# Batched float32 matmul on one core: the first pair's loads in 8 KB runs, and no small store beside them

## The chip, the core and the metric

The kernel runs on one core of one Trainium2 chip. The metric is the device time of one execution, in microseconds (us). Before the change it was 124.75 us (median of 3 runs, 124.73 to 124.80). PE is the matrix engine and PEld its weight loads, ACT and DVE are the scalar and vector engines, POOL is a further engine, which only clears memory here, and SP is the engine that issues most DMAs here. "The DMA engines" are the 16 engines that move data for the core.

## The reference, cut to what matters

```python
batch, m, k, n = 16, 512, 512, 512          # a: (16, 512, 512), b: (16, 512, 512), float32
np.matmul(a.transpose(0, 2, 1), b)          # out: (16, 512, 512), float32
```

Two inputs of 16.8 MB are read and one output of 16.8 MB is written: 50.3 MB, none of it twice.

## The kernel before

Two batches make a pair, and there are eight pairs. A load brings one pair of a, or of b, as 2 MB: each of 128 partitions gets 16 KB that lie together in memory. DVE casts to bf16, PE multiplies into its result memory (PSUM), ACT copies PSUM to an output tile, and SP stores it, 2 MB at a time in 8 KB runs. SP issues all sixteen loads first and the eight stores after them. On ACT's queue there is one small store of 64 KB at the beginning; its place in the output is written again later.

```python
    with tc.tile_critical(no_gpsimd_drain=True):
        for n in range(2 * pairs):                      # a0, b0, a1, b1, ...
            if n >= NX:                                 # NX = 4 load buffers
                nc.sync.wait_ge(s_in, n - NX + 1)
            nc.sync.dma_start(x_ts[n % NX][:], in_v[n % 2][n // 2]).then_inc(s_x[n % NX], 16)
        nc.sync.wait_ge(s_w, 16)
        for i in range(pairs):
            nc.sync.wait_ge(s_out, i + 1)
            nc.sync.dma_start(out_v[i], o_ts[i % NO][:]).then_inc(s_o if i else s_o0, 16)
        # ... final waits; DVE casts; PE loop over pairs ...
        nc.gpsimd.memset(o_ts[0][:, 0, 0, 0:P], 0.0).then_inc(s_z, 1)
        nc.scalar.wait_ge(s_z, 1)
        nc.scalar.dma_start(out_v[0][:, 0, 0, 0:P], o_ts[0][:, 0, 0, 0:P]).then_inc(s_w, 16)
        nc.scalar.wait_ge(s_w, 16)
        # ... ACT copies PSUM to o_ts ...
```

Of the kernel before, what the change touches and what calls it, by code (L numbers as in the profile page):

```python
# [1 line left out]

# [4 lines left out]

@with_exitstack
def kernel(
    ctx: ExitStack,  # L10
    tc: tile.TileContext,
    a: bass.AP,
    b: bass.AP,
    out: bass.AP,
):
    nc = tc.nc
    P = 128
    batch, K, M = a.shape
    _, _, N = b.shape
    f32 = mybir.dt.float32  # L20
    bf = mybir.dt.bfloat16




    G = 2
    Q = P // G
    R = K // Q
    V = 2
    RV = R // V  # L30
    T = M // P
    H = T // 2
    pairs = batch // G
    in_v = [x.rearrange("(pair g) (q r) m -> pair (g q) r m", g=G, r=R) for x in (a, b)]
    out_v = out.rearrange("(pair g) (c t) n -> pair c g t n", g=G, t=T)

    NX = 4
    NO = pairs - 1



    pool = ctx.enter_context(tc.tile_pool(name="sb", bufs=1))
    psum = ctx.enter_context(tc.tile_pool(name="ps", bufs=1, space=bass.MemoryType.PSUM))
    x_ts = [pool.tile([P, R, M], f32, name=f"x{j}") for j in range(NX)]
    abf_ts = [pool.tile([P, RV, M], bf, name=f"abf{v}") for v in range(V)]
    bbf_ts = [pool.tile([P, RV, N], bf, name=f"bbf{v}") for v in range(V)]
    o_ts = [pool.tile([P, G, T, N], f32, name=f"o{j}") for j in range(NO)]
    dve_done = pool.tile([1, 2 * pairs], f32, name="dve_done")
    act_done = pool.tile([1, pairs], f32, name="act_done")
    ps_ts = [[psum.tile([P, 2, N], f32, name=f"ps{g}{h}") for h in range(H)] for g in range(G)]  # L50

    s_x = [tc.alloc_semaphore(f"s_x{j}") for j in range(NX)]
    s_o0 = tc.alloc_semaphore("s_o0")
    s_o = tc.alloc_semaphore("s_o")
    s_w = tc.alloc_semaphore("s_w")
    s_z = tc.alloc_semaphore("s_z")
    s_in = tc.alloc_semaphore("s_in")
    s_cast = tc.alloc_semaphore("s_cast")
    s_v = tc.alloc_semaphore("s_v")
    s_mm = tc.alloc_semaphore("s_mm")  # L60
    s_ev = [tc.alloc_semaphore(f"s_ev{h}") for h in range(H)]
    s_out = tc.alloc_semaphore("s_out")

    with tc.tile_critical(no_gpsimd_drain=True):  # L64
        for n in range(2 * pairs):
            if n >= NX:
                nc.sync.wait_ge(s_in, n - NX + 1)
            nc.sync.dma_start(x_ts[n % NX][:], in_v[n % 2][n // 2]).then_inc(s_x[n % NX], 16)
        nc.sync.wait_ge(s_w, 16)
        for i in range(pairs):  # L70
            nc.sync.wait_ge(s_out, i + 1)
            nc.sync.dma_start(out_v[i], o_ts[i % NO][:]).then_inc(s_o if i else s_o0, 16)
        nc.sync.wait_ge(s_o0, 16)
        nc.sync.wait_ge(s_o, 16 * (pairs - 1))

        for i in range(pairs):
            for v in range(V):
                if i and v == 0:
                    nc.vector.wait_ge(s_v, G * i)
                if i and v == 1:  # L80
                    nc.vector.wait_ge(s_mm, G * H * i)
                for n in (2 * i, 2 * i + 1):
                    if v == 0:
                        nc.vector.wait_ge(s_x[n % NX], 16 * (n // NX + 1))
                    nc.vector.tensor_copy(  # L85
                        out=(bbf_ts if n % 2 else abf_ts)[v][:],
                        in_=x_ts[n % NX][:, v * RV:(v + 1) * RV, :],
                    ).then_inc(s_cast, 1)
                    if v == V - 1:

                        nc.vector.memset(dve_done[:, n:n + 1], 0.0).then_inc(s_in, 1)  # L91

        for h in range(H):
            nc.tensor.sem_inc(s_ev[h], 1)
        with nc.tensor.Fori(0, pairs):
            for v in range(V):
                nc.tensor.wait_ge(s_cast, 2).then_inc(s_cast, -2)
                for t in range(T):
                    h = t // 2
                    if v == 0 and t % 2 == 0:  # L100
                        nc.tensor.wait_ge(s_ev[h], 1).then_inc(s_ev[h], -1)  # L101
                    for r in range(RV):
                        for g in range(G):
                            rows = slice(g * Q, (g + 1) * Q)
                            a_m = abf_ts[v][rows, r, :].rearrange("p (c t) -> p t c", t=T)
                            mm = nc.tensor.matmul(  # L106
                                ps_ts[g][h][:, t % 2, :],
                                a_m[:, t],
                                bbf_ts[v][rows, r, :],
                                start=(v == 0 and r == 0),  # L110
                                stop=(v == V - 1 and r == RV - 1),
                            )
                            if v == 0 and t == T - 1 and r == RV - 1:
                                mm.then_inc(s_v, 1)
                            if v == V - 1 and t % 2 and r == RV - 1:
                                mm.then_inc(s_mm, 1)


        nc.gpsimd.memset(o_ts[0][:, 0, 0, 0:P], 0.0).then_inc(s_z, 1)  # L119
        nc.scalar.wait_ge(s_z, 1)  # L120
        nc.scalar.dma_start(out_v[0][:, 0, 0, 0:P], o_ts[0][:, 0, 0, 0:P]).then_inc(s_w, 16)
        nc.scalar.wait_ge(s_w, 16)
        for i in range(pairs):
            if i == NO:
                nc.scalar.wait_ge(s_o0, 16)
            for h in range(H):
                for g in range(G):
                    nc.scalar.wait_ge(s_mm, G * H * i + G * h + g + 1)  # L128
                    ev = nc.scalar.copy(  # L129
                        out=o_ts[i % NO][:, g, 2 * h:2 * h + 2, :], in_=ps_ts[g][h][:]  # L130
                    )
                ev.then_inc(s_ev[h], 1)

            nc.scalar.memzero(act_done[:, i:i + 1]).then_inc(s_out, 1)  # L134


# [1 line left out]
_INS = ['a', 'b']  # L138
_OUTS = [((16, 512, 512), 'float32')]


# [23 lines left out]
```

## Time and profile before

| what | value | view |
|---|---|---|
| time, median | 124.75 us | runs |
| span of the profiled execution | 122.8 us | page |
| DMA queue of SP, share of 16 engines' span | 96.9% | queue table |
| PE, DVE, ACT busy | 49%, 31%, 26% | busy table |
| last work of PE, DVE or ACT | ends near 93 us | chain of waits |

The page of the kernel before. The first two rows cut the span into 40 slices: busy tenths of the DMA engines, and what they moved. Then the DMA queues, with packets, MB and share.

```profile
DMA  4999999999999999999999999999999999999992
GB/s 85 386 415 437 432 437 443 427 432 437 427 432 427 427 427 427 427 427 427 427 427 427 427 427 427 427 416 427 424 427 427 427 427 427 427 427 427 429 432 101
...
q1 hardware_dynamic: 4480, 50.33, 96.9%
q10 hardware_dynamic: 144, 0.07, 0.2%
```

The DMA engines are full from the second slice to the last but one; this is the bound. The Trainium skill, "DMA: Bandwidth & Descriptors", section "Where 436 GB/s comes from", puts the ceiling at 435.2 GB/s; the 427 of most slices agree with it. So an engine that computes faster would bring nothing. What can still move are the two ends, and what each DMA engine has to carry.

The start of the kernel before, as windows. The columns are the stretch, its length, busy time with count for PE, PEld, DVE, ACT and POOL, granted clock, DMA share and GB/s.

```profile
1.00:2.00 1.00, 0.00 (x0) 0.00 (x0) 0.00 (x0) 0.00 (x0) 0.15 (x1) 1.00 0.24 49
2.00:3.00 1.00, 0.00 (x0) 0.00 (x0) 0.00 (x0) 0.00 (x0) 0.00 (x0) 1.00 0.98 180
3.00:4.00 1.00, 0.00 (x0) 0.00 (x0) 0.00 (x0) 0.00 (x0) 0.00 (x0) 1.00 0.73 262
4.00:6.00 2.00, 0.00 (x0) 0.00 (x0) 0.00 (x0) 0.00 (x0) 0.00 (x0) 1.00 1.00 426
```

Between 2 and 4 us the engines have work but move little: the first packets are slow. And the start of the timeline of the kernel before (start, duration, engine, line, operation; in brackets how long the engine sat idle before, and what ended that):

```profile
0.94 0.39 SPq L68 DMA_DIRECT2D x<-in_a_dram  x1
1.18 0.37 ACTq L121 DMA_DIRECT2D out_dram<-o  x1
...
8.90 1.23 DVE L85 CAST abf<-x 128x2048 bf16<-128x2048 f32 x1 [8.90 <-DMA x<-in_a_dram]
13.79 1.23 DVE L85 CAST bbf<-x 128x2048 bf16<-128x2048 f32 x1 [3.66 <-DMA x<-in_b_dram]
```

The trace also holds one record for every DMA packet: start, duration, size and queue. It does not name the DMA engine. But each DMA ends on every engine with a 4-byte write to its semaphore, so each DMA has 16 such writes, one for each engine. This gives, after each DMA, when the last engine got there. For the end of the kernel these are the 16 writes of the last store. In before, the last one starts at 121.05 us. The records show the time from one packet to the next on an engine: 607 ns with 16 KB loads, 306 ns with 8 KB stores, and 630 ns where a 512-byte packet of the small store lies between two 16 KB packets.

### The profile page before, as it was taken

Reading aid. Unit: us, or ns where it says so; the run is one execution under the profiler, and the core shown is the slowest. Engines: PE = TensorE matmul, PEld = TensorE weight load, DVE = VectorE, ACT = ScalarE, POOL = GpSimd, SP = SyncE. Lnnn points to the kernel's source line nnn. Section 1 sums busy time; section 2 is a strip of 40 time slices with the busy share of each in tenths; the row PEclk is TensorE's granted clock in tenths of the full one; section 3 lists DMA queues with packets and bytes.
Section 4 is the critical chain, followed back from the end, with each engine's and each line's share of the span. In section 5 each row is a group of like instructions: output and inputs, shape, how many; then the busy total and the mean of one; then the engine's idle time right before and its main releaser. Section 6 shows DMA issues by size and latency. Waiting matters only on the chain. (4 is left out here: it accounts for less than half of the span.)

```text
span 122.8 us, 1258 instructions
## 1 busy us (share of the span) xinstructions
PE 60.2 (49%) x512; PEld 35.4 (29%) x512; DVE 37.9 (31%) x48; ACT 31.8 (26%) x41; POOL 0.4 (0%) x5
## 2 busy tenths in 40 slices
PE   0000099859769649829919928997960000000000
PEld 0000045436446336416606604544630000000000
DVE  0012562583294094174355337239000000000000
ACT  0000000690740830650570390065093000000000
POOL 1000000000000000000000000000000000000000
PEclk9999999999999999999999995999998555555555
DMA  4999999999999999999999999999999999999992
GB/s 85 386 415 437 432 437 443 427 432 437 427 432 427 427 427 427 427 427 427 427 427 427 427 427 427 427 416 427 424 427 427 427 427 427 427 427 427 429 432 101
DMA packets 4624, 50.40 MB, mean 410 GB/s; under 512 B 400, under 2 KB 528, under 8 KB 528
## 3 DMA queue, kind: packets, MB, share of 16 engines
q1 hardware_dynamic: 4480, 50.33, 96.9%
q10 hardware_dynamic: 144, 0.07, 0.2%
HBM read 33.55 MB, written 16.84 MB: 410 GB/s over the span
## 5 line engine op out<-in xcount | busy, mean ns | idle before, releaser
L106 PE MATMUL ps<-bbf,abf 64*128 64x512 bf16 x512 | 60.2, 392 | 30.7 <-PEq L101 29.0
L106 PEld LDWEIGHTS ps<-bbf,abf 64*128 64x128 bf16 x512 | 35.4, 112 | 55.1 <-issue 38.2
L129 ACT COPY o<-ps 128x1024 f32<-128x1024 f32 x32 | 30.1, 1027 | 38.7 <-PE ps L106 38.7
L85 DVE CAST abf<-x 128x2048 bf16<-128x2048 f32 x16 | 19.6, 1223 | 25.1 <-PE ps L106 16.2
L85 DVE CAST bbf<-x 128x2048 bf16<-128x2048 f32 x16 | 19.6, 1224 | 22.9 <-DMA x<-in_b_dram 22.9
L129 ACT ACT_TABLE_LOAD x1 | 1.3, 1283 | 22.6 <-PE ps L106 22.6
L134 ACT ACTIVATE act_done<-act_done 1x1 uint32<-1x1 uint32 x8 | 1.6, 197 | 0.0
L91 DVE MEMSET dve_done<- 1x1 f32 x16 | 0.9, 59 | 0.0
L119 POOL MEMSET o<- 128x128 f32 x1 | 0.2, 204 | 0.5 <-SPq L64 0.5
L149 POOL MEMSET const-bfloat16-1.0<- 128x1 bf16 x1 | 0.1, 102 | 0.0
L149 POOL MEMSET const-uint8-127<- 128x1 uint8 x1 | 0.1, 101 | 0.0
L149 POOL MEMSET const-float32-0.0<- 128x1 f32 x1 | 0.1, 98 | 0.2 <-issue 0.2
L149 POOL MEMSET const-float32-1.0<- 128x1 f32 x1 | 0.1, 98 | 0.0
## 6 DMA issues: line engine op xcount, KB each, us to landing
x<-in_a_dram SPq DMA_DIRECT2D x8, 2048.0 KB, 12.2
x<-in_b_dram SPq DMA_DIRECT2D x8, 2048.0 KB, 16.0
out_dram<-o SPq DMA_DIRECT2D x8, 2048.0 KB, 30.6
out_dram<-o ACTq DMA_DIRECT2D x1, 64.0 KB, 9.0
```

The costliest lines, as they stand in the source:

```text
L85: nc.vector.tensor_copy(out=(bbf_ts if n % 2 else abf_ts)[v][:], in_=x_ts[n % NX][:, v * RV:(v + 1) * RV, :],).then_inc(s_cast, 1)
L91: nc.vector.memset(dve_done[:, n:n + 1], 0.0).then_inc(s_in, 1)
L106: mm = nc.tensor.matmul(ps_ts[g][h][:, t % 2, :], a_m[:, t], bbf_ts[v][rows, r, :], start=(v == 0 and r == 0), stop=(v == V - 1 and r == R ...
L119: nc.gpsimd.memset(o_ts[0][:, 0, 0, 0:P], 0.0).then_inc(s_z, 1)
L129: ev = nc.scalar.copy(out=o_ts[i % NO][:, g, 2 * h:2 * h + 2, :], in_=ps_ts[g][h][:])
L134: nc.scalar.memzero(act_done[:, i:i + 1]).then_inc(s_out, 1)
L149: nc = _bacc.Bacc("TRN2", target_bir_lowering=False, num_devices=1)
```

## The change

The intent: take the small store's packets out of the way of the first loads, and let the first loads come in shorter packets.

```diff
-            nc.sync.dma_start(x_ts[n % NX][:], in_v[n % 2][n // 2]).then_inc(s_x[n % NX], 16)
-        nc.sync.wait_ge(s_w, 16)
+            if n < 2:
+                for v in range(V):                      # V = 2 halves of RV = 4 rows
+                    r = slice(v * RV, (v + 1) * RV)
+                    nc.sync.dma_start(x_ts[n][:, r, :], in_v[n][0][:, r, :]).then_inc(s_x[n], 16)
+            else:
+                nc.sync.dma_start(x_ts[n % NX][:], in_v[n % 2][n // 2]).then_inc(s_x[n % NX], 16)
...
-                        nc.vector.wait_ge(s_x[n % NX], 16 * (n // NX + 1))
+                        nc.vector.wait_ge(s_x[n % NX], 16 * (n // NX + 1 + (n % NX < 2)))
...
-        nc.gpsimd.memset(o_ts[0][:, 0, 0, 0:P], 0.0).then_inc(s_z, 1)
-        nc.scalar.wait_ge(s_z, 1)
-        nc.scalar.dma_start(out_v[0][:, 0, 0, 0:P], o_ts[0][:, 0, 0, 0:P]).then_inc(s_w, 16)
-        nc.scalar.wait_ge(s_w, 16)
```

(The two semaphores s_w and s_z go as well.)

More of the change, by code (lines that the diff above doesn't have):

```diff
@@ L54 @@
     s_o = tc.alloc_semaphore("s_o")
-    s_w = tc.alloc_semaphore("s_w")
-    s_z = tc.alloc_semaphore("s_z")
     s_in = tc.alloc_semaphore("s_in")
```

## The prediction

> **What bounds the kernel now.** The DMA engines. The page's slices show DMA at 9 tenths or more from the second slice to the last but one, at 386 to 443 GB/s; the queue table gives the SP queue 96.9% of 16 engines' span, against 49% for PE and 31% for DVE. In 4 us windows from 4 to 120 us the rate stays within 406 to 455 GB/s, through loads and stores (from about 81 us) alike. The Trainium skill ("DMA: Bandwidth & Descriptors", Where 436 GB/s comes from) puts the ceiling at 435.2 GB/s; the trace agrees, with about 427. PE, DVE and ACT are done by 93 of 122.8 us. So only three things matter: when the DMA engines start, what each moves, and what it loses on the way.
>
> **An engine's budget, from the trace's packet records.** First packets start at 1.98 to 2.5 us (first issue at 0.94). In steady state a 16 KB load packet follows its predecessor after 607 ns, an 8 KB store packet after 306 ns, a 4-byte semaphore write takes about 6 ns: 128 x 607 + 128 x 306 + 24 x 6 = 117.0 us. The engines end at 120.4 to 121.1. The remaining 1.3 us or so lie in the first 4 us: the first 16 KB packets take 0.9 to 2.0 us instead of 0.61, some second ones 0.7 to 1.1, and the window from 3 to 4 us moves only 262 GB/s at a DMA share of 0.73.
>
> **What the change does.**
> 1. Small store gone: 128 packets of 512 B, 8 per engine. From 4.7 us they alternate with load packets (the same page, Queues, rings and completion order: round-robin by packet) and stretch the interval from 607 to 630 ns. 8 x 23 = 0.18 us saved on every engine, all critical. The waits for it cost nothing now: it landed at about 10 us; ACT's first copy starts at 23.9 us, SP's first store issue is at 66.8.
> 2. First pair in 8 KB packets: per engine 32 packets for 16. At 306 against 303.5 ns that costs 16 x 4.5 = 0.07 us, plus 2 more semaphore writes, 0.01 us. SP issues 6 DMAs instead of 4, about 0.45 us each, but the queue is 15 us ahead.
> 3. Start-up: first packets half as long, so an engine that fills its pipe packet by packet may lose up to 0.3 us less. I count 0.15 us, the uncertain term.
> 4. The casts do not start earlier than about 8.6 us (8.9 before): the first still waits for both halves of a. Not critical.
>
> Sum: -0.18 + 0.08 - 0.15 = -0.25 us.
>
> **Prediction: 124.5 us**, 8 in 10 between 124.0 and 124.9. Chances: faster by over 2% 0.01, within 2% 0.98, slower by over 2% 0.01.
>
> **What would show it.** The ACT queue (q10) gone from the queue table; intervals of 607 or 2 x 306 ns between 4 and 10 us and no 512 B packets; first packets ending earlier, and the window 3 to 4 us above 262 GB/s; last packets at about 120.8 instead of 121.1 us; the later rate unchanged. Step 3 is wrong if no more bytes have moved by 5 us than before.
>
> **What would make it wrong.** If the small store warmed the write path, the first real stores near 81 us show packets well over 306 ns, and up to about 1 us comes back. If the three engines that end 0.35 us after the rest get later by start-up luck, the saving vanishes; likewise if half-row reads are slower at the start. A large effect needs a change of the steady rate; I see no cause.

## The result, and the profile after

The changed kernel took 124.79 us (median of 6 runs, 124.64 to 124.86), and before 124.78 us (6 runs). The ratio is 1.000, with a 95% interval from 0.9987 to 1.0013. A ratio here is the mean time of one kernel's fast runs over the mean of the other's in the same rounds, so it is not quite the ratio of the medians. The time lies inside the predicted range, but so would that of a kernel that changes nothing; the predicted quarter of a microsecond is not there.

The page of the changed kernel, the same rows:

```profile
DMA  3999999999999999999999999999999999999991
GB/s 77 406 427 427 440 432 438 427 427 438 427 432 427 427 427 432 432 427 427 432 438 427 427 427 427 427 398 427 424 430 427 427 430 427 430 430 427 427 432 59
...
q1 hardware_dynamic: 4768, 50.33, 96.9%
```

ACT's queue is gone, SP's has 288 packets more (256 more of data, 32 more of semaphore writes), and the last slice moves 59 instead of 101 GB/s: most engines finish earlier. The windows and the timeline of the start of the changed kernel:

```profile
1.00:2.00 1.00, 0.00 (x0) 0.00 (x0) 0.00 (x0) 1.00 (x1) 0.00 (x0) 1.00 0.06 16
2.00:3.00 1.00, 0.00 (x0) 0.00 (x0) 0.00 (x0) 0.18 (x1) 0.00 (x0) 1.00 0.92 197
3.00:4.00 1.00, 0.00 (x0) 0.00 (x0) 0.00 (x0) 0.00 (x0) 0.00 (x0) 1.00 0.92 360
4.00:6.00 2.00, 0.00 (x0) 0.00 (x0) 0.00 (x0) 0.00 (x0) 0.00 (x0) 1.00 1.03 430
```

```profile
0.94 0.87 SPq L70 DMA_DIRECT2D x<-in_a_dram  x2
...
8.50 1.23 DVE L88 CAST abf<-x 128x2048 bf16<-128x2048 f32 x1 [8.50 <-DMA x<-in_a_dram]
13.47 1.23 DVE L88 CAST bbf<-x 128x2048 bf16<-128x2048 f32 x1 [3.75 <-DMA x<-in_b_dram]
```

What was predicted for the start is there. The window from 3 to 4 us moves 360 instead of 262 GB/s, and the first cast starts 0.40 us earlier. (The prediction's own test, more bytes moved by 5 us, says little: 1.00 against 0.99 MB, counted by packets started, and a packet is 8 or 16 KB on each of 16 engines.) Most of the lead is kept. From the packet records, the mean engine's semaphore write, and the last engine's:

| after which DMA | before: mean, last | changed: mean, last |
|---|---|---|
| a of pair 0 | 8.09, 8.52 us | 7.72, 8.08 us |
| b of pair 0 | 13.01, 13.43 us | 12.62, 12.99 us |
| last load | 81.41, 81.83 us | 81.09, 81.52 us |
| last store | 120.64, 121.05 us | 120.31, 121.05 us |

The mean engine ends 0.33 us earlier. The last engine ends at the same moment as before. It still was 0.31 us ahead after the last load, so it lost this among the stores. The packet records show where: from about 84 to 91 us one engine's store packets, one after the other, take 313 to 342 ns instead of 309 (343 ns in sum), and in this trace that engine is already the latest one. In before the same happens (26 packets, 351 ns in sum), but there it falls on an engine that was not late, only brings it level with two that were, and costs next to nothing.

**Theory S.** The time follows the last of the 16 DMA engines. The change helps the mean engine as predicted, but the spread between the engines takes part of it back. **Theory P**, part of it: the slow packets near the end come from the last pair's matmuls, which run from 83.55 to 90.65 us. **Rival C.** The two parts of the change cancel on every engine: the 8 KB packets cost as much as the store's removal saves.

### The profile page after: what moved, and what is told of

Same layout as the page of the kernel before. It is cut to its first block, busy times and chain, and to the rows that moved or that the text cites. A ratio compares the mean times of both kernels' runs of the same rounds, so it can differ in the third digit from the quotient of the medians.

```text
span 122.8 us, 1254 instructions
## 1 busy us (share of the span) xinstructions
PE 62.9 (51%) x512; PEld 36.0 (29%) x512; DVE 38.0 (31%) x48; ACT 31.8 (26%) x41; POOL 0.2 (0%) x4
## 5 line engine op out<-in xcount | busy, mean ns | idle before, releaser
L109 PE MATMUL ps<-bbf,abf 64*128 64x512 bf16 x512 | 62.9, 405 | 27.7 <-PEq L104 27.7
L109 PEld LDWEIGHTS ps<-bbf,abf 64*128 64x128 bf16 x512 | 36.0, 114 | 54.1 <-issue 38.1
```

Source lines behind the costliest of these rows:

```text
L109: mm = nc.tensor.matmul(ps_ts[g][h][:, t % 2, :], a_m[:, t], bbf_ts[v][rows, r, :], start=(v == 0 and r == 0), stop=(v == V - 1 and r == R ...
```

## The experiments

Twelve runs were made, of ten different kernels. Each was timed in 5 rounds, with before run in the same rounds on the same chip.

### 1. Only the store removed

```diff
-        nc.gpsimd.memset(...); nc.scalar.wait_ge(s_z, 1)
-        nc.scalar.dma_start(out_v[0][:, 0, 0, 0:P], ...).then_inc(s_w, 16)
-        nc.scalar.wait_ge(s_w, 16)            # and SP's wait for s_w
```

> The kernel before without the small store; first loads in 16 KB packets as before. Theory S (slowest engine): every DMA engine saves 8 x 23 = 0.18 us, so the median engine's last packet goes from 120.56 to about 120.38 us, but the time follows the slowest engine, which is 0.5 us behind the median in before and 0.8 in after; time 124.5 to 124.8. Rival C (the two parts cancel: the store's removal saves 0.18 us, the 8 KB packets cost as much): 124.60 us, clearly below before.

Measured: 124.47 us against 124.72 of before, ratio 0.9983 (0.9970 to 0.9996). The mean engine ended at 120.52 us (before: 120.64), the last at 120.69, only 0.17 us behind it. The time does not separate the two accounts, and the expectation missed one number: the median engine ended at 120.56 us, as in before, and not at 120.38.

> The kernel without the small store, 16 KB first loads, once more, beside the changed kernel on the same chip. So far 124.47 us against 124.72 of before. If that gain is the store's (about 0.2 us on every DMA engine): 0.2 us below before again, mean of the engines' last packets near 120.5 us.

Measured, on another chip: 124.59 us against 124.77, ratio 0.9989 (0.9975 to 1.0002); mean engine 120.50, last 120.95 us. The mean of the two ratios is 0.9986, which is 0.17 us, with an uncertainty of some 0.12 us by the two intervals. This agrees with the predicted 0.18. The mean engine gained less, 0.12 us, so the agreement is in part luck.

### 2. Only the 8 KB runs

The changed kernel with the store, its memset and its waits put back.

> The changed kernel with the small store put back (8 KB packets for the first pair, and the store). Theory S: median engine's last packet at about 120.23 + 0.18 = 120.41 us, i.e. 0.15 us before that of the kernel before; time 124.7 to 125.0, by the slowest engine. Rival C: 8 KB packets cost 0.18 us, median engine at about 120.75 us, time 124.97 us.

Measured: 124.83 us against 124.72, ratio 1.0008 (0.9995 to 1.0021). The 8 KB runs alone do not help; if anything they cost 0.1 us, but the interval holds 1, no change at all. In the trace the median engine ended at 120.70 us, near Rival C's 120.75 and not Theory S's 120.41, and a's last packets came at 8.11 us on the mean engine, not earlier than in before (8.09): beside the store the 8 KB runs gained nothing at the start. The profiled run is also the slowest of the five (125.17 us), so this trace may not be a typical one.

### 3. Four small stores instead of one

```diff
-        nc.scalar.dma_start(out_v[0][:, 0, 0, 0:P], o_ts[0][:, 0, 0, 0:P]).then_inc(s_w, 16)
+        for t in range(T):                    # T = 4
+            nc.scalar.dma_start(out_v[0][:, 0, t, 0:P], o_ts[0][:, 0, t, 0:P]).then_inc(s_w, 16)
```

> The kernel before with four such small stores instead of one (512 packets of 512 B, 32 per engine). If a packet of the store costs every engine 23 ns of its own time: 24 x 23 = 0.55 us more on all engines, median engine at about 121.1 us, time about 125.3 us. If the store hides behind the loads or the time does not come from the DMA engines: 124.8 us.

The queue lines of this kernel:

```profile
q1 hardware_dynamic: 4480, 50.33, 96.4%
q10 hardware_dynamic: 576, 0.26, 0.7%
```

Measured: the mean engine ends at 121.20 us, 0.56 later than before, where 0.55 was expected. That match is in part luck: after the fifth load the mean engine was 0.67 us behind that of before, and 0.11 us came back because the loads of this kernel stayed at 4.862 us each until 42.9 us, those of before until 27.6 (section 7). The cost of a packet itself is seen beside the first loads: 5.057 instead of 4.862 us for a load with about 8 small packets on each engine, so some 24 ns each. The time was 125.59 us, though, 0.87 above before. The missing 0.3 us or so lie outside the span of the profile: in all five runs the time is 2.28 to 2.34 us above the span, and in before's runs 1.91 to 2.03. What that is stays open.

### 4. The changed kernel without the last pair's matmuls

This gives a wrong result for the last pair. ACT waits for DVE's last cast instead.

```diff
-        with nc.tensor.Fori(0, pairs):
+        with nc.tensor.Fori(0, pairs - 1):
```

> The changed kernel without the matmuls of the last pair (wrong result for that pair on purpose; DVE and ACT work stay). In before and after one engine's store packets take 314 to 342 ns instead of 309 from about 84 to 91 us, the time of the last pair's matmuls, and in after this makes the last engine end at 121.05 instead of about 120.7 us. Theory P (the matmuls beside the stores cause it): no packet above 316 ns after 84 us, last engine less than 0.55 us behind the median, time about 124.45 us. Rival Q (it comes from the stores themselves, or from SP's issues): slow packets stay, time 124.8 us.

The timelines, first of the changed kernel and then of this one, around the last pair (PE, DVE and ACT lines):

```profile
83.17 1.22 DVE L88 CAST abf<-x 128x2048 bf16<-128x2048 f32 x1
83.55 7.10 PE L109 MATMUL ps<-bbf,abf 64*128 64x512 bf16 x64 [2.69 <-PEq L104]
...
88.99 3.76 ACT L127 COPY o<-ps 128x1024 f32<-128x1024 f32 x4 [6.03 <-PE ps L109]
```

```profile
83.25 1.22 DVE L88 CAST abf<-x 128x2048 bf16<-128x2048 f32 x1
84.39 1.22 DVE L88 CAST bbf<-x 128x2048 bf16<-128x2048 f32 x1
...
86.97 3.76 ACT L130 COPY o<-ps 128x1024 f32<-128x1024 f32 x4 [3.94 <-DMA out_dram<-o]
```

DVE's casts and ACT's copies still run beside the stores (ACT's copies 2 us earlier); the matmuls are gone. Slow store packets after 83.5 us (more than 312 ns): 1, of 6 ns excess, where the changed kernel has 25, with 343 ns in sum. The last engine ended 0.31 us behind the mean instead of 0.73. Theory P holds: with the last pair's matmuls, one DMA engine loses about a third of a microsecond, and without them none does. All 13 traces with these matmuls, of every kernel, show it (21 to 26 slow packets one after the other, 316 to 351 ns in sum). How matmuls do this, and why to one engine only, is open. The smaller spread alone would not prove it: without its 343 ns the last engine of the changed kernel's first trace would have been about 0.4 us behind, and in this kernel it is 0.31. The median time was 124.55 us, 0.1 above what was expected: in this run the start had been slower (a at 7.89 us).

### 5. The changed kernel twice more

> The changed kernel once more. If the 8 KB runs give back what the store's removal saves: equal to before within 0.1 us, 0.2 to 0.3 us above the kernel without the store. Theory S says why: the engines' mean is not later than without the store (120.3 to 120.5 us), but the last engine is 0.5 to 0.8 us behind the mean, against 0.17 us there. If that was luck of one trace: both kernels' last engine about as far behind, and times within 0.1 us of each other.

> The changed kernel a third time, for its times beside these and for one more trace of its spread: mean engine's end 120.3 to 120.4 us, the last engine 0.4 to 0.8 us behind it, time 3.70 us after the last engine's last packet, as in all traces but that of four stores; 124.65 to 124.8 us.

Measured: 124.64 us against 124.77 (ratio 0.9988, 0.9976 to 1.0001) and 124.69 against 124.74 (0.9998, 0.9985 to 1.0011), on two further chips. The mean engine ended at 120.41 and 120.44 us, the last at 120.87 and 120.91, so 0.46 and 0.47 us behind. The 0.73 us of the first trace were partly luck. The first of these two runs has the kernel without the store (124.59 us, ratio 0.9989, last engine 0.44 us behind) in the same rounds on the same chip: the times are equal within 0.05 us, and both last engines are about as far behind. By the expectation's own words that is the outcome "luck of one trace". Over the three measurements the mean ratio is 0.9995: the change brings 0.06 us, and the store's removal alone 0.17. The difference of 0.11 us is smaller than its uncertainty, some 0.15 us by the intervals.

### 6. One DMA engine given more work

An extra load of 17 partitions x 2 KB on ACT's queue, added to the kernel without the store. The Trainium skill, "DMA: Bandwidth & Descriptors", section "Why a DMA increments its semaphore by 16 and not by 1", says that a DMA runs on the largest number of engines up to 16 that divides its slowest dimension; for 17 that is one.

```diff
+        nc.scalar.dma_start(o_ts[0][0:17, 0, 0, :], in_v[0][0][0:17, 0, :]).then_inc(s_w, 16)
+        nc.scalar.wait_ge(s_w, 16)
```

> The kernel without the small store, with one extra load of 17 partitions x 2 KB on ACT's queue. 17 rows do not divide over engines, so by the Trainium skill (DMA: Bandwidth & Descriptors, on why a DMA increments its semaphore by 16) all 17 packets should run on one DMA engine: about 17 x 80 ns = 1.4 us more there, nothing on the other 15. Theory S (the time is the last packet of the last engine plus 3.70 us): that engine ends up to 1.4 us later than it would, the mean engine only 0.09 us; time 0.6 to 1.4 us above the kernel without the store, i.e. 125.1 to 125.9 us. Rival (the time follows the total work of the 16 engines): 0.09 us more, 124.6 us. If the packets turn out spread over the engines, the test is void.

The queue line and the issue line of this load:

```profile
q10 hardware_dynamic: 18, 0.03, 0.1%
...
o<-in_a_dram ACTq DMA_DIRECT2D x1, 34.0 KB
```

There is one semaphore write, so one engine, as the page says; its packets follow each other 80 ns apart, and later 687 ns apart with a 16 KB packet between them (607 + 80). Measured: 125.20 us against 124.83 of before, ratio 1.0031 (1.0016 to 1.0047). The mean engine ended at 120.56 us, only 0.05 later than in the two runs without this load; the last one ended at 121.38, 0.83 behind the mean. The time is some 0.6 us above the kernel without the store, although 15 engines have nothing to do with it. Followed packet by packet, the engine with the extra load is the one that ended last. The time is at the low end of what was expected. A likely reason, not tested: 15 of the 17 packets ran before 3.6 us, while the first load packets of the other engines were slow as well (they ended between 3.0 and 3.9 us). Theory S holds, and its rival (0.09 us) falls.

### 7. How the 8 KB packets cost, and what they gain at the start

Every load in 8 KB runs:

```diff
-            if n < 2:                         # and no else branch
```

> The changed kernel with every load in 8 KB runs, two DMAs of 1 MB each. If the cost of the 8 KB runs is one of packets and semaphore writes (a 2 MB load takes 4.908 us as two DMAs of 8 KB packets, 4.862 us as one of 16 KB, while PE is idle): seven more pairs cost up to 7 x 0.09 = 0.65 us, time up to 125.4 us; less if loads beside running matmuls (4.89 us) hide it. If the cost is one of start-up alone: no change against the changed kernel, 124.8 us.

Measured: 125.79 us, ratio 1.0077 (1.0064 to 1.0090), 1.15 us above the changed kernel's median of the same rounds. The windows from 20 to 60 us, first of the changed kernel (the run of the same rounds), then of this one:

```profile
20.00:60.00 40.00, 33.43 (x288) 19.42 (x286) 20.27 (x25) 15.61 (x21) 0.00 (x0) 0.96 1.00 427
```

```profile
20.00:60.00 40.00, 32.08 (x278) 19.48 (x274) 20.17 (x25) 15.26 (x20) 0.00 (x0) 0.96 1.01 422
```

Early on, 2 MB as two DMAs of 8 KB packets take 4.906 us instead of 4.862; later 4.97 instead of 4.893. The first is what I had predicted for the first pair (0.08 us for both loads). The second I had not seen, and 14 loads x 0.075 = 1.05 us is about what the mean engine lost (121.50 against 120.41, so 1.09). The expectation put the slower rate down to matmuls beside the loads, but that does not fit: in before and in the kernel with four stores matmuls start at 15.3 us, while the loads stay at 4.862 us until 27.6 us in the one and 42.9 us in the other. With 8 KB runs the slower rate begins earlier, near 20 us for the changed kernel. What sets it off is open.

Still shorter packets at the start, in three ways: the first pair in 4 KB runs; or only the first part of the first load in 4 KB or 2 KB runs and the rest as in the kernel without the store.

```diff
+            if n == 0:                        # 2: 4 KB, then 12 KB; 1: 2 KB, then 14 KB
+                for r in (slice(0, 2), slice(2, R)):
+                    nc.sync.dma_start(x_ts[n][:, r, :], in_v[n][0][:, r, :]).then_inc(s_x[n], 16)
```

> The changed kernel with the first pair in 4 KB runs, four DMAs of 512 KB for each of a and b. If shorter first packets shorten the start (my step 3): the mean engine has a's last packet no later than in the changed kernel (7.7 to 7.9 us), and more bytes moved by 4 us. If per-packet cost rules: b's last packet 0.1 to 0.3 us later than in the changed kernel (12.6 to 12.8 us), time 124.9 to 125.1 us.

> No small store; the first load (a of pair 0) as 512 KB in 4 KB packets and then 1.5 MB in 12 KB packets, everything after it in 16 KB packets. In the run with 4 KB packets for the whole first pair, a's last packets came 0.55 us earlier on the mean engine than with 16 KB packets (7.44 against 7.99 us), though each 2 MB in 4 KB packets costs 0.37 us more in steady state. If the gain is made by the very first packets alone, most of it is kept without that cost: a at 7.2 to 7.5 us, mean engine's end 119.9 to 120.1 us, time 123.9 to 124.3 us. If the start loses time until the packets are large, or the gain needs small packets throughout: a at 7.8 us or later, time 124.4 to 124.7 us.

(The 7.44 us quoted there was misread: it is the third of the four DMAs of a. The last one came at 8.68 us, and the 0.37 us hold a second slow stretch, told below; without it 2 MB in 4 KB packets cost 4 x 1.248 - 4.862 = 0.13 us. So the ramp was built on a wrong reading.)

> The same with 256 KB in 2 KB packets and 1.75 MB in 14 KB packets. If shorter first packets go on helping: a at 7.1 to 7.4 us, time 123.8 to 124.2 us. If the pipe fills anew with the first 14 KB packet: like the kernel without the store, a at 7.9 to 8.0 us, time 124.55 us.

| first load | a of pair 0, mean engine | time | ratio to before |
|---|---|---|---|
| 16 KB, no store (two runs) | 8.01, 7.97 us | 124.47, 124.59 us | 0.9983, 0.9989 |
| 8 KB, changed kernel (three runs) | 7.72, 7.71, 7.70 us | 124.79, 124.64, 124.69 us | 1.0000, 0.9988, 0.9998 |
| 4 KB for the pair | 8.68 us | 125.68 us | 1.0072 |
| 4 KB, then 12 KB | 8.14 us | 125.02 us | 1.0022 |
| 2 KB, then 14 KB | 8.42 us | 125.05 us | 1.0017 |

So in these runs, all without the store, 8 KB gains 0.28 us at the start against 16 KB, and anything shorter loses. (The two other kernels that start with 8 KB and no store, without the last matmuls and with all loads in 8 KB, had a at 7.89 and 7.85 us; over all five the gain is 0.22 us.) This refutes my reason for the gain, an engine that fills its pipe packet by packet: by it, 4 KB would have gained more, but already the first 1 MB came later than with 8 KB (5.67 against 5.25 us on the mean engine). In the run with 4 KB the packets were slow a second time, from 5.4 to 7.4 us (up to 654 ns instead of 159), and a third time near 9 us. A 512 KB DMA that otherwise took 1.248 us then took 1.768 and 1.485. The windows of the 4 KB run show it too:

```profile
4.00:6.00 2.00, 0.00 (x0) 0.00 (x0) 0.00 (x0) 0.00 (x0) 0.00 (x0) 1.00 0.99 373
6.00:8.00 2.00, 0.00 (x0) 0.00 (x0) 0.00 (x0) 0.00 (x0) 0.00 (x0) 1.00 0.97 332
8.00:10.00 2.00, 0.00 (x0) 0.00 (x0) 0.34 (x1) 0.00 (x0) 0.00 (x0) 1.00 1.02 377
```

Why is open, and so is why 8 KB starts best.

### What all traces say together

| kernel | mean engine's end | last engine's end | time of that run | time minus last | time minus mean |
|---|---|---|---|---|---|
| before | 120.64 | 121.05 | 124.79 | 3.74 | 4.15 |
| changed | 120.31 | 121.05 | 124.76 | 3.72 | 4.45 |
| changed, second | 120.41 | 120.87 | 124.55 | 3.68 | 4.14 |
| changed, third | 120.44 | 120.91 | 124.63 | 3.72 | 4.19 |
| no store | 120.52 | 120.69 | 124.39 | 3.70 | 3.87 |
| no store, second | 120.50 | 120.95 | 124.62 | 3.67 | 4.12 |
| store and 8 KB | 120.71 | 121.43 | 125.17 | 3.74 | 4.46 |
| all 8 KB | 121.50 | 122.16 | 125.89 | 3.73 | 4.39 |
| one engine loaded | 120.56 | 121.38 | 125.08 | 3.70 | 4.52 |

All numbers are us; differences are taken from unrounded ends. The time is 3.67 to 3.74 us after the last engine's last packet, in these nine traces and in those of the kernels without last matmuls, with 4 KB, and with the two ramps (3.68 to 3.73); only the kernel with four stores has 4.10. Time minus mean, in contrast, wanders over 0.65 us. What counts is when the last engine ends.

## Why the prediction was right or wrong, point by point

- **The bound.** Right. DMA engines fill the span, and the first cast that starts 0.40 us earlier does not show in the time.
- **Step 1, the store: 0.18 us.** Right in size as far as the runs resolve it: 0.17 us alone. With 8 KB runs in place, the mean ratio goes from 1.0008 to 0.9995, some 0.16 us. Four stores cost the mean engine 0.56 us, where 0.55 was expected, in part by luck.
- **Step 2, 8 KB packets: 0.08 us.** Right for the two loads of the first pair: 2 x (4.906 - 4.862) = 0.09 us.
- **Step 3, start-up: 0.15 us.** Without the store the gain exists, and was larger: 0.22 us on the mean engine when a has landed, over five runs, and this already has the cost of a's packets in it. In the one trace of 8 KB runs beside the store there was none (8.11 against 8.09 us). The reason given for it is refuted by the 4 KB and 2 KB runs.
- **Step 4.** Right: the first cast started at 8.50 us, and nothing came of it.
- **The warm write path.** Right that the store did not serve to warm anything: the first stores of the changed kernel, near 81 us, take 309 to 316 ns.
- **The sum, and what failed in it.** "Sum: -0.18 + 0.08 - 0.15 = -0.25 us" is a sum for the mean engine, and there it is what happened: 120.39 us over three traces, against 120.64 in the one trace of before. The step that failed took this to be the time. The time is the last engine's: it ended at 121.05, 120.87 and 120.91 us, against 121.05, so 0.11 us earlier in the mean, and the time fell by 0.06 us.

  How far the last engine is behind has two sources. One is the spread from the start, the other the delay of one engine by the last matmuls. In the traces the last engine is 0.46 to 0.73 us behind the mean with 8 KB runs (the three changed ones, the one with the store, the one with all loads), against 0.17 to 0.44 with 16 KB (before, the two without a store, and the four stores). That looks as if 8 KB runs drove the engines apart, but it is not shown. The ranges are 0.01 us apart, and the kernel without the last matmuls has 8 KB runs and 0.31. After the last load, before the matmuls' delay falls, the same traces give 0.36 to 0.57 us with 8 KB and 0.19 to 0.46 with 16 KB, which overlap.

  So the 8 KB runs, without the store, put the mean engine 0.12 us ahead (120.39 against 120.51), and none of that is seen in the time (mean ratio 0.9995 against 0.9986; in the same rounds 0.9988 against 0.9989). Rival C, that the parts cancel on each engine, is not what the changed kernel's traces show; the one trace with store and 8 KB runs is close to it.
- **The risk that was named.** "If the three engines that end 0.35 us after the rest get later by start-up luck, the saving vanishes" is close to what came, with one thing missing: the delay of one engine by the last matmuls. Where it falls on a late engine (the changed kernel's first trace, and the one with store and 8 KB), a third of a microsecond is lost. As far as the packets can be followed from one to the next, the delayed engine is the last one in six of the 13 traces, where it costs between 0.02 and 0.35 us (0.13 in the changed kernel's third), and in the other seven it costs nothing.

What stays open: whether the 8 KB runs set the engines further apart at all, or whether chance did in these few traces, and with that where the mean engine's 0.12 us went. More runs of the changed kernel and the one without the store in the same rounds would tell. Whether the delayed engine is the same one in each run cannot be read, as the records do not name engines.

The best version that ran is the one with the store removed and the 16 KB loads kept, at 124.47 and 124.59 us. Its mean ratio of 0.9986 to before is 0.17 us, 0.11 us better than the changed kernel's 0.9995; that is less than the intervals resolve, and in the rounds that both shared they were equal.

## What to carry to other kernels

In a kernel bound by DMA, add up the costs for each DMA engine, but read the time from the last engine: the 16 semaphore writes of the last DMA show how far it is behind. Work taken from all engines alike (here a needless small store) can be expected in the time, and 0.17 us of it was seen; a gain of the mean engine need not be, because one late engine sets the time: 0.34 us of delay on one engine undid it in the changed kernel's first trace. When two changes come together, run each alone, and each more than once: here one trace each put the last engine 0.17 and 0.73 us behind the mean, and a second one 0.44 and 0.46.

## What the Trainium skill lacked or had wrong

- "DMA: Bandwidth & Descriptors", "Why small descriptors are slow (HBM only)", gives a fixed overhead for each packet as about 3 cycles, without a clock. The runs show 4.6 ns in the early loads, at every size: 16 KB follows after 607 ns, 8 KB after 306, 4 KB after 155, 2 KB after 80, and 512 bytes add 23; all fit 4.6 ns plus the bytes at 27.2 GB/s for one engine. Later in the run (from about 18 us in the kernel with all loads in 8 KB), cutting 16 KB in two costs some 9 ns instead.
- The same page, "Queues, rings and completion order", says that an engine goes round its queues by packet, and the traces agree, but it gives no cost: small packets of ACT's queue alternated with 16 KB packets of SP's, which then followed each other 630 ns apart instead of 607.
- No page that I read tells of the cold start: the first 16 KB packets took 0.9 to 2.0 us instead of 0.61. With 16 KB packets the load of a ended at 8.0 us, with 8 KB at 7.7, with 4 KB at 8.7.
- No page that I read says that the 16 engines largely keep the spread they start with: 0.42 us between mean and last after the first load of before, and 0.42 us after the last load (in the changed kernel's three traces 0.37, 0.49 and 0.49 after the load of a, and 0.43, 0.48 and 0.36).
- "SBUF — State Buffer", "SBUF: two separate sides", says that a compute instruction cannot slow a DMA. Here matmuls did: beside stores one DMA engine lost some 0.33 us in 25 packets (1 slow packet without those matmuls). It is small, about 14 ns for a packet of 309.
- No page that I read tells of the slower rate later in the run: a 2 MB load takes 4.862 us at first and 4.893 later, from about 28 us in before. Its cause was not found.
